# A batched matmul with scale and add: the weight loaded by GpSimd's queue, and GpSimd's DMAs as single packets

## The chip, the core and the metric

The kernel runs on one core of one Trainium2 chip. The metric is the device time in microseconds (us) of one execution; the lower the better. Three runs of the kernel before took 206.86 to 207.15 us, median 207.01 us.

A core has engines that run side by side and meet at semaphores: PE (TensorE, the matmuls), DVE (VectorE), ACT (ScalarE), POOL (GpSimd) and SP (SyncE, which here only issues DMAs). DMAs are carried out by 16 DMA engines that all queues share. A transfer that SP issues goes into one queue (hardware_dynamic in the profile), a transfer that POOL issues into another (software_dynamic). Each DMA engine moves packets; a transfer over 128 partitions is dealt out to the 16 engines.

## What is computed

```python
batch, m, k, n = 16, 512, 1024, 768
out = scale * np.matmul(x, weight) + add_value      # all float32
```

x is 16 x 512 x 1024, weight 1024 x 768, add_value and the result 16 x 512 x 768. Flattened, x has 8192 rows: 64 tiles of 128 rows. The core reads 32 MB of x, 3 MB of weight and 24 MB of addend, and writes 24 MB.

## The kernel before

**Tiles.** A tile t is 128 rows, one on each partition. Four tiles make a *move*; 16 tiles stand in the x buffer `xs` (X_SLOTS), 32 in `ao` (A_SLOTS), which holds the addend of a tile, then its result, until it is stored. At the start the weight lies in float32 in slots 24 to 31 of `ao` (W_AT), which no addend needs yet.

**SP** issues every large DMA in the order of the list `STREAM` (L22 to L29): "x" loads of x, "a" of the addend, "w" of the weight, "o" stores; the numbers are first tile and count. The first x load (tiles 0 to 7, 4 MB) is issued ahead of that, at L239. `sync_engine` (L97) walks the list and puts waits before an entry where it must:
- an x load into used slots waits until ACT and POOL have cast what stood there (`by_act`, `by_pool`, L116 and L117);
- an addend load waits for the addend load before it (`a_sem`, L122). The load of tiles 40 to 47 also waits for `aside_sem` (L126), since slots 8 and 15 of `ao` hold the results of tiles 8 and 15 until POOL has stored them;
- a store waits until DVE has made its tiles (`made`, L142).

SP takes one entry after the other, so a wait holds up all that stand behind it. The weight is issued as two transfers of 1.5 MB, four of the eight chunks of 128 weight rows each. On one partition one such transfer consists of two runs of 6144 bytes, so it has 256 runs, 16 for each DMA engine. An x load of eight tiles is one run of 32768 bytes on a partition, an addend load of eight tiles one of 24576.

**ACT and POOL** run `mover` (L150): they wait for a move's x (L156), wait until a `va` buffer is free (`turned`), and cast x to bfloat16 into `va`, 8 instructions each for a move. Before its loop for moves 0 to 7, POOL does nothing. Between moves 7 and 8 it waits until 16 tiles are made (L246) and issues the three stores of `BY_POOL` by `store_pair` (L93): tiles 8 and 15, of 6, 98 and 24 partitions, each partition two runs of 3072 bytes.

**DVE** (`vector_engine`) first casts the two halves of the weight to bfloat16 (L171), each as soon as it has landed, then transposes the first move (L178). In its loop it alternates between finishing two tiles (L187: scale times product plus addend, in place in `ao`) and transposing half a move into `xt`. A transpose waits for both ACT's and POOL's casts of that move (L175, L176).

**PE** waits for both weight casts (L222) and then goes through the tiles, 16 matmuls each (L210), as fast as `xt` is filled and the results are taken out.

Of the kernel before, what the change touches and what calls it, by code (L numbers as in the profile page):

```python
# [16 lines left out]
VA_BUFS = 2  # L17
MOVE = 4
AHEAD = 4
HALF_BLOCK, PAST, SYNC_AT = 64, 4, 4  # L20

STREAM = [  # L22
# [8 lines left out]
PAIR, TURN_AT = slice(8, 16, 7), 2  # L31
# [4 lines left out]
def kernel(  # L36
# [8 lines left out]
    nc = tc.nc  # L45
# [14 lines left out]
    out_v = out_f.rearrange("(g p t) n -> p g t n", p=P, t=R)  # L60
    w_v = weight.rearrange("(c p r) n -> p c (r n)", p=P, r=2)

    def rows(view, s, n):
        assert s // R == (s + n - 1) // R
        return view[:, s // R, s % R:s % R + n, :]
# [5 lines left out]
    ao = const.tile([P, A_SLOTS, N], fp32, name="ao")  # L71
# [6 lines left out]
    w_sem = [tc.alloc_semaphore(f"w{i}") for i in range(2)]  # L78
    x_sem = [tc.alloc_semaphore(f"x{i}") for i in range(X_SLOTS // MOVE)]
    a_sem = tc.alloc_semaphore("a")  # L80
    o_sem = [tc.alloc_semaphore(f"o{i}") for i in range(2)]
    aside_sem = tc.alloc_semaphore("aside")
# [5 lines left out]
    W_AT = A_SLOTS - KJ  # L88

    def slot(t):  # L90
        return t % A_SLOTS

    def store_pair(eng, p, n):  # L93
        assert PAIR.stop <= R and PAIR.stop <= A_SLOTS
        eng.dma_start(out_v[p:p + n, 0, PAIR, :], ao[p:p + n, PAIR, :]).then_inc(aside_sem, 16)  # L95

    def sync_engine(eng):  # L97
        groups, stores, known = 0, [], {}

        def need(sem, value):  # L100
            if known.get(sem, 0) < value:
                eng.wait_ge(sem, value)  # L102
                known[sem] = value

        for at, (op, s, n) in enumerate(STREAM):
            if at == SYNC_AT:
                eng.addr_align(HALF_BLOCK, offset=PAST, max_nops=0)
            last = s + n - 1
            if op == "w":
                dst = ao[:, W_AT + s:W_AT + s + n, :].rearrange("p (c r) n -> p c (r n)", r=2)  # L110
                move, sem = eng.dma_start(dst, w_v[:, s // 2:(s + n) // 2, :]), w_sem[s // 4]
            elif op == "x":
                k = s % X_SLOTS
                if last >= X_SLOTS:
                    moved = 8 * (last + 1 - X_SLOTS) // MOVE
                    need(by_act, moved)  # L116
                    need(by_pool, moved)  # L117
                move = eng.dma_start(xs[:, k:k + n, :], rows(x_v, s, n))  # L118
                sem = x_sem[k // MOVE]
            elif op == "a":  # L120
                if groups:
                    need(a_sem, 16 * groups)  # L122
                if last == A_SLOTS - 1:
                    need(casts, KJ)
                if s <= PAIR.start + A_SLOTS <= last:
                    need(aside_sem, 16 * len(BY_POOL))  # L126
                if s >= A_SLOTS:
                    i = next(j for j, (a, b) in enumerate(stores) if a <= last - 1 - A_SLOTS < a + b)
                    need(o_sem[i % 2], 16 * (i // 2 + 1))
                move = eng.dma_start(ao[:, slot(s):slot(s) + n, :], rows(add_v, s, n))  # L130
                sem = a_sem
                groups += 1
            elif op == "a+":
                need(a_sem, 16 * groups)
                eng.sem_inc(a_sem, 16 * (n // G - 1))
                groups += n // G - 1
                continue
            else:
                i = len(stores)
                if i > 1:  # L140
                    need(o_sem[i % 2], 16 * (i // 2))
                need(made, MADE + last + 1)  # L142
                move = eng.dma_start(rows(out_v, s, n), ao[:, slot(s):slot(s) + n, :])
                sem = o_sem[i % 2] if s < ENDING else end_sem
                stores.append((s, n))
            move.then_inc(sem, 16)
            if op == "x" and n == 2 * MOVE:
                eng.sem_inc(x_sem[k // MOVE + 1], 16)

    def mover(eng, copy, parity, count, go=None, first=0, turns=T // X_SLOTS):  # L150
        if go is None:
            eng.preload_act_table(mybir.ActivationFunctionType.Copy)  # L152
        with eng.Fori(16 * (first + 1), 16 * (first + turns) + 1, 16) as i:  # L153
            for q in range(X_SLOTS // MOVE):
                eng.wait_ge(x_sem[q], i)
                eng.wait_ge(turned, i + (4 * q - 12) if q < 3 else i)  # L156
                if go is not None:
                    eng.sem_inc(go, 1)  # L158
                k = MOVE * q
                src = xs[:, k:k + MOVE, :].rearrange("p i (c b k) -> p (i c) b k", b=4, k=64)  # L160
                for a in (parity, parity + 2):
                    for b in range(4):
                        copy(va[q % VA_BUFS][32 * b:32 * b + 32, :, a, :],  # L163
                             src[32 * a:32 * a + 32, :, b, :]).then_inc(count, 1)

    def vector_engine(eng):
        ao_g = ao.rearrange("p (g t) n -> p g t n", t=G)

        def cast_w(s, n):
            eng.wait_ge(w_sem[s // 4], 16)  # L170
            eng.tensor_copy(w_bf[:, s:s + n, :], ao[:, W_AT + s:W_AT + s + n, :]).then_inc(casts, n)  # L171

        def turn(move, half, moves=None):
            if half == 0:
                eng.wait_ge(by_act, moves)  # L175
                eng.wait_ge(by_pool, moves)  # L176
            q = 2 * half * KC
            eng.transpose(  # L178
                xt[:, 2 * half:2 * half + 2, :, :].rearrange("p i c m -> p (i c m)"),
                va[move % VA_BUFS][:, q:q + 2 * KC, :, :].bitcast(fp32).rearrange("p c a k -> p (c a k)"),  # L180
            ).then_inc(turned, 2)

        def finish(pair, at, products):
            eng.wait_ge(done, products)
            a = ao_g[:, at, 2 * pair:2 * pair + 2, :]
            q = 2 * (pair % 2)
            eng.scalar_tensor_tensor(  # L187
                a, mm[:, q:q + 2, 0:N], float(scale), a,
                op0=mybir.AluOpType.mult, op1=mybir.AluOpType.add).then_inc(made, 2)

        def group(i, at, last):
            eng.wait_ge(a_sem, i)
            for p in range(4):
                finish(p, at, i + (4 * p - 12) if p < 3 else i)
                if p < 2 or not last:
                    turn(1 if p < 2 else 0, p % 2, i + 8 if p == 2 else i)

        cast_w(0, 4)
        cast_w(4, 4)
        turn(0, 0, 8)  # L200
        turn(0, 1)
        with eng.Fori(16, 2 * T, 16) as i:
            group(i, bass.ds((i // 16 + A_SLOTS // G - 1) % (A_SLOTS // G), 1), False)
        s = slot(T - G) // G
        group(2 * T, slice(s, s + 1), True)
# [12 lines left out]
    def tensor_engine(eng):  # L218
        eng.sem_inc(x_sem[1], 16)
        eng.sem_inc(turned, TURNED)  # L220
        eng.sem_inc(made, MADE)
        eng.wait_ge(casts, KJ)  # L222
        with eng.Fori(TURNED + 2, TURNED + 2 + T, XT_TILES) as i:
            for q in range(XT_TILES):
                if q % 2 == 0:
                    eng.wait_ge(turned, i + q if q else i)
                    eng.wait_ge(made, i + q if q else i)
                for j in range(KJ):
                    x2 = xt[:, q, j // 2, :].bitcast(bf16).rearrange("p (m r) -> p r m", r=2)
                    m = product(eng, mm[:, q, :], x2[:, j % 2, :], w_bf[:, j, :], j)  # L230
                if q % 2:
                    m.then_inc(done, 4)
# [4 lines left out]
    s, n = FIRST  # L237
# [4 lines left out]
    with tc.tile_critical(no_gpsimd_drain=True):  # L242
        sync_engine(nc.sync)
        mover(nc.scalar, nc.scalar.copy, 0, by_act)
        mover(nc.gpsimd, nc.gpsimd.tensor_copy, 1, by_pool, pool_go, 0, TURN_AT)
        nc.gpsimd.wait_ge(made, MADE + PAIR.stop)  # L246
        for p, n in BY_POOL:
            store_pair(nc.gpsimd, p, n)
        nc.gpsimd.addr_align(HALF_BLOCK, offset=PAST, max_nops=0)
        mover(nc.gpsimd, nc.gpsimd.tensor_copy, 1, by_pool, pool_go, TURN_AT, T // X_SLOTS - TURN_AT)  # L250
        vector_engine(nc.vector)
        tensor_engine(nc.tensor)
# [40 lines left out]
```

## Time and profile before

| | us |
|---|---|
| median of 3 runs | 207.01 |
| the profiled execution | 206.85 |
| its span (first to last instruction) | 205.5 |
| PE busy | 167.5 |
| POOL busy | 137.4 |
| ACT busy | 134.7 |
| DVE busy | 98.0 |

HBM traffic is 87.04 MB, 424 GB/s over the span. The times in the views that follow are counted from the start of the span. An engine's busy time is the sum of its instructions. In the lists of DMA issues the last number is the time from issue to landing, which holds the time that a transfer stands in its queue. The chain of waits follows back what released each step, from the last instruction of the program.

### The profile page before, as it was taken

To read this page: it belongs to the slowest core of one execution; us is meant where nothing else is said; L and a number is where in the kernel's file an instruction comes from. 1 tells how busy PE (TensorE), PEld (TensorE's weight loads), DVE (VectorE), ACT (ScalarE), POOL (GpSimd) and SP (SyncE) were. 2 spreads that over 40 slices of the span, in tenths; PEclk is the share of its full clock that TensorE was granted. 3 is DMA by queue.
4 is the path that set the end of the run, shared out by engine and by line. 5 is a ranking of instruction groups with operands and counts; after the bars stand their busy time and mean duration, and the time that the engine had idled before them with its cause. 6 is when DMAs were issued, how large, how long until landed. Compare 5 with 4: busy or idle time off the path is not lost.

```text
span 205.5 us, 2223 instructions
## 1 busy us (share of the span) xinstructions
PE 167.5 (82%) x1008; PEld 50.4 (25%) x512; DVE 98.0 (48%) x66; ACT 134.7 (66%) x129; POOL 137.4 (67%) x135
## 2 busy tenths in 40 slices
PE   0000099999999999999999999999999997999900
PEld 0000022233322333223332233332333322333200
DVE  0004525537555555465555555555552853455330
ACT  2049980699999906999999059999991099920000
POOL 0049994699999916999999549999992099930000
PEclk9999999999999999999999999999999999999995
DMA  8989999999999899999999999999999999998997
GB/s 287 427 372 438 440 485 408 392 437 459 446 459 459 357 459 408 408 426 413 455 404 450 431 416 464 434 411 421 440 431 415 437 448 421 493 459 364 423 440 304
DMA packets 4065, 87.04 MB, mean 424 GB/s; under 512 B 480, under 2 KB 480, under 8 KB 1120
## 3 DMA queue, kind: packets, MB, share of 16 engines
q1 hardware_dynamic: 3856, 86.25, 98.1%
q0 software_dynamic: 208, 0.79, 0.9%
q14 instruction: 1, 0.01, 0.0%
HBM read 61.87 MB, written 25.17 MB: 424 GB/s over the span
## 4 chain that ended last, share of the span: by engine, by line
DMA 38%; PE 36%; POOL 10%; ACT 5%; issue 4%; DVE 3%; SPq 1%; POOLq 0%; DVEq 0%; ACTq 0%
PE mm L210 36%; DMA out_dram<-ao 22%; DMA xs<-in_x_dram 15%; POOL va L163 9%; ACT va L163 5%; DVE xt L178 2%; DVE ao L187 1%; POOL out_dram L95 1%; SPq L130 0%; SPq L118 0%; DVEq L176 0%; SPq L102 0%; POOLq L156 0%; POOLq L158 0%; POOLq L153 0%
## 5 line engine op out<-in xcount | busy, mean ns | idle before, releaser
L210 PE MATMUL mm<-w_bf,xt 128*128 128x256 bf16 (+1 forms) x1008 | 167.5, 327 | 28.0 <-DVE xt L178 27.1
L163 POOL CAST va<-xs 32x1024 bf16<-32x1024 f32 x128 | 135.2, 1056 | 44.2 <-DMA xs<-in_x_dram 36.8
L163 ACT CAST va<-xs 32x1024 bf16<-32x1024 f32 x128 | 133.4, 1042 | 45.2 <-DMA xs<-in_x_dram 42.2
L187 DVE SCALAR_TENSOR_TENSOR ao<-mm,ao 128x1536 f32 (+1 forms) x32 | 56.2, 1756 | 72.9 <-PE mm L210 68.9
L208 PEld LDWEIGHTS <-xt 128*128 128x128 bf16 x512 | 50.4, 98 | 144.6 <-issue 116.6
L178 DVE STREAM_TRANSPOSE xt<-va 128x1024 f32<-128x1024 f32 x32 | 39.4, 1234 | 8.4 <-POOL va L163 6.3
L171 DVE CAST w_bf<-ao 128x3072 bf16<-128x3072 f32 x2 | 4.5, 2240 | 18.1 <-DMA ao<-in_weight_dram 18.1
L152 ACT ACT_TABLE_LOAD x1 | 1.3, 1283 | 1.3 <-SPq L242 1.3
L95 POOL DMA_DIRECT2D out_dram<-ao x3 | 2.0, 672 | 0.0
L274 POOL MEMSET const-float32-0.0<- 128x1 f32 x1 | 0.1, 98 | 0.2 <-issue 0.2
L274 POOL MEMSET const-bfloat16-1.0<- 128x1 bf16 x1 | 0.1, 101 | 0.0
L274 POOL MEMSET const-float32-1.0<- 128x1 f32 x1 | 0.1, 98 | 0.0
L274 POOL MEMSET const-uint8-127<- 128x1 uint8 x1 | 0.1, 98 | 0.0
## 6 DMA issues: line engine op xcount, KB each, us to landing
xs<-in_x_dram SPq DMA_DIRECT2D x7, 4096.0 KB, 20.9
ao<-in_add_value_dram SPq DMA_DIRECT2D x6, 3072.0 KB, 15.7
out_dram<-ao SPq DMA_DIRECT2D x3, 3072.0 KB, 27.4
ao<-in_add_value_dram SPq DMA_DIRECT2D x1, 6144.0 KB, 24.2
out_dram<-ao SPq DMA_DIRECT2D x1, 6144.0 KB, 31.2
out_dram<-ao SPq DMA_DIRECT2D x1, 4608.0 KB, 14.9
xs<-in_x_dram SPq DMA_DIRECT2D x2, 2048.0 KB, 21.0
ao<-in_weight_dram SPq DMA_DIRECT2D x2, 1536.0 KB, 16.8
```

The lines of the kernel that those rows point to most:

```text
L95: eng.dma_start(out_v[p:p + n, 0, PAIR, :], ao[p:p + n, PAIR, :]).then_inc(aside_sem, 16)
L152: eng.preload_act_table(mybir.ActivationFunctionType.Copy)
L163: copy(va[q % VA_BUFS][32 * b:32 * b + 32, :, a, :], src[32 * a:32 * a + 32, :, b, :]).then_inc(count, 1)
L171: eng.tensor_copy(w_bf[:, s:s + n, :], ao[:, W_AT + s:W_AT + s + n, :]).then_inc(casts, n)
L178: eng.transpose(xt[:, 2 * half:2 * half + 2, :, :].rearrange("p i c m -> p (i c m)"), va[move % VA_BUFS][:, q:q + 2 * KC, :, :].bitcast(fp ...
L187: eng.scalar_tensor_tensor(a, mm[:, q:q + 2, 0:N], float(scale), a, op0=mybir.AluOpType.mult, op1=mybir.AluOpType.add).then_inc(made, 2)
L208: eng.ldweights(x_j, tile_position=(0, 0))
L210: m = eng.add_instruction(mybir.InstMatmult(start_tensor_calc=(j == 0), stop_tensor_calc=(j == KJ - 1), tile_size=(P, P), tile_position=(0 ...
L274: nc = _bacc.Bacc("TRN2", target_bir_lowering=False, num_devices=1)
```

## The change

SP's list loses its two weight entries. POOL issues the same two transfers to the same places, at the head of its program: after it has seen the first x load land, and before its first cast. Both of them, and the three stores of tiles 8 and 15, carry a flag, `single_packet`, that asks for one packet on each DMA engine that a transfer uses. `SYNC_AT`, a position in the list at which SP's code is aligned, moves with the list by two, so that it stays at the same entry.

```diff
-HALF_BLOCK, PAST, SYNC_AT = 64, 4, 4
+HALF_BLOCK, PAST, SYNC_AT = 64, 4, 2

 STREAM = [
-    ("w", 0, 4), ("w", 4, 4), ("a", 0, 8),
+    ("a", 0, 8),
     ("x", 8, 8), ("a", 8, 8), ("x", 16, 8), ("a", 16, 16), ("x", 24, 8),
...
     def store_pair(eng, p, n):
         assert PAIR.stop <= R and PAIR.stop <= A_SLOTS
-        eng.dma_start(out_v[p:p + n, 0, PAIR, :], ao[p:p + n, PAIR, :]).then_inc(aside_sem, 16)
+        eng.dma_start(out_v[p:p + n, 0, PAIR, :], ao[p:p + n, PAIR, :], single_packet=True).then_inc(aside_sem, 16)
+
+    def load_weight(eng):
+        for s in (0, 4):
+            dst = ao[:, W_AT + s:W_AT + s + 4, :].rearrange("p (c r) n -> p c (r n)", r=2)
+            eng.dma_start(dst, w_v[:, s // 2:s // 2 + 2, :], single_packet=True).then_inc(w_sem[s // 4], 16)
...
-            if op == "w":
-                dst = ao[:, W_AT + s:W_AT + s + n, :].rearrange("p (c r) n -> p c (r n)", r=2)
-                move, sem = eng.dma_start(dst, w_v[:, s // 2:(s + n) // 2, :]), w_sem[s // 4]
-            elif op == "x":
+            if op == "x":
...
         mover(nc.scalar, nc.scalar.copy, 0, by_act)
+        nc.gpsimd.wait_ge(x_sem[0], 16)
+        load_weight(nc.gpsimd)
         mover(nc.gpsimd, nc.gpsimd.tensor_copy, 1, by_pool, pool_go, 0, TURN_AT)
```

## The prediction

> **What bounds the kernel now.** I read the table of DMA queues first, because section 2 of the page shows the DMA row at 9 in nearly every slice. Its columns are packets, MB and share of 16 engines' span.
>
> ```profile
> q1 hardware_dynamic: 3856, 86.25, 98.1%
> q0 software_dynamic: 208, 0.79, 0.9%
> out_dram<-ao SPq DMA_DIRECT2D x1, 6144.0 KB, 31.2
> out_dram<-ao SPq DMA_DIRECT2D x1, 4608.0 KB, 14.9
> ao<-in_weight_dram SPq DMA_DIRECT2D x2, 1536.0 KB, 16.8
> out_dram<-ao POOLq DMA_DIRECT2D x1, 588.0 KB, 15.1
> out_dram<-ao POOLq DMA_DIRECT2D x1, 144.0 KB, 18.7
> out_dram<-ao POOLq DMA_DIRECT2D x1, 36.0 KB, 7.4
> ```
>
> The two data queues together fill 99.0% of the 16 engines. The bytes set the time, as long as SP's queue never runs dry. The other lines are issues with their time to landing. Next, the timeline of the start: what do the first 26 us wait for? Columns: start, length, engine, line, instruction, and in brackets the idle time before it.
>
> ```profile
> 0.74 0.38 SPq L239 DMA_DIRECT2D xs<-in_x_dram  x1
> 1.39 0.90 SPq L111 DMA_DIRECT2D ao<-in_weight_dram  x2
> 12.89 17.04 ACT L163 CAST va<-xs 32x1024 bf16<-32x1024 f32 x16 [10.26 <-DMA xs<-in_x_dram]
> 13.04 20.27 POOL L163 CAST va<-xs 32x1024 bf16<-32x1024 f32 x16 [12.60 <-DMA xs<-in_x_dram]
> 16.65 2.31 DVE L171 CAST w_bf<-ao 128x3072 bf16<-128x3072 f32 x1 [16.65 <-DMA ao<-in_weight_dram]
> 20.40 2.17 DVE L171 CAST w_bf<-ao 128x3072 bf16<-128x3072 f32 x1 [1.44 <-DMA ao<-in_weight_dram]
> 24.69 2.37 DVE L178 STREAM_TRANSPOSE xt<-va 128x1024 f32<-128x1024 f32 x2 [2.12 <-ACT va L163]
> 26.00 34.27 PE L210 MATMUL mm<-w_bf,xt 128*128 128x512 bf16 x197 [26.00 <-DVE xt L178]
> 27.64 0.33 SPq L130 DMA_DIRECT2D ao<-in_add_value_dram  x1
> 33.41 0.33 SPq L118 DMA_DIRECT2D xs<-in_x_dram  x1
> 37.44 23.45 ACT L163 CAST va<-xs 32x1024 bf16<-32x1024 f32 x22 [7.51 <-DMA xs<-in_x_dram]
> 44.67 0.33 SPq L130 DMA_DIRECT2D ao<-in_add_value_dram  x1
> ```
>
> Transfers land in order: x of move 0 and 1 at 12.8, the weight halves at 16.6 and 20.4, tiles 0 to 7 of the addend at 27.6 (SP waits for them before it issues at 27.64), x 8 to 15 at 37.4. PE starts at 26.0, behind a transpose that waited for casts, not for the weight: DVE was idle for 2.12 us after the second weight cast. So the weight may land about 2 us later before PE moves.
>
> The waits of PE from 150 us on show one single stall, and the timeline of the end (DVE, then PE, then SP) says where PE's progress meets the queue.
>
> ```profile
> PE mm L210 <- DVE xt L178: 1.1, 1, 1.1
> 185.17 1.76 DVE L187 SCALAR_TENSOR_TENSOR ao<-mm,ao 128x1536 f32<-128x1536 f32 x1 [1.98 <-PE mm L210]
> 174.49 20.97 PE L210 MATMUL mm<-w_bf,xt 128*128 128x512 bf16 x126 [1.13 <-DVE xt L178]
> 159.64 38.10 SPq L143 DMA_DIRECT2D out_dram<-ao  x3
> ```
>
> Store 32-47 is issued at 159.64 and lands 31.2 later, at 190.84. Store 48-59 needs tile 59, which DVE makes at 185.17 + 1.76 = 186.93. It is issued 3.9 us before the queue would run dry. That is the smallest reserve in the kernel: all later bytes hang on it, and PE's progress sets it.
>
> **The change, part by part.**
>
> *Fewer packets.* The second weight half took 20.40 − 16.65 = 3.75 us in the hardware queue; the addend tiles behind it, of twice its bytes in packets of 24 KB, took 27.64 − 20.40 = 7.24, or 3.62 per 1.5 MB. I put the 0.13 us between them down to 16 packets of 6 KB per engine (256 runs over 16 engines) instead of one: 9 ns a packet. Two halves give −0.26. The stores of tiles 8 and 15 go from up to 10 data packets on an engine to 3: −0.06. Sum **−0.32 us** of engine time; 0 if the cost is one per run and not per packet, which is the other end.
>
> *Two transfers leave SP's queue.* SP issues the addend at about 1.4 instead of 2.3 us, behind an x load that keeps the engines busy to 12.8: nothing. The same bytes must pass before 27.6 either way, so the addend's landing stays, and with it the issue at 27.64. If it came late, x 8 to 15, landing at 37.4, covers 9.7 us.
>
> *Two issues on POOL.* The wait on x_sem[0] is the one its first cast has already, so it adds no time. Behind it stand both transfers and then the 16 casts of moves 0 and 1.
>
> ```profile
> L95 POOL DMA_DIRECT2D out_dram<-ao x3: 596/693/727, 96.2 to 97.6; - x3
> L163 POOL CAST va<-xs x10: 1026/1034/2452, 13.0 to 25.7; 32x1024 bf16<-32x1024 f32 x10
> ```
>
> One issue takes 0.60 to 0.73 us, hardly more for 98 partitions than for 6. So POOL's casts start 1.4 us later. Alone that would push PE from 26.0 to about 27.4. The slots that they free go to the x load issued at 33.41; it would go at 34.8, with cover up to 44.67, when the addend before it lands.
>
> *When the weight lands.* This decides. Three facts come from the one place where POOL stores while SP's queue is full. These are tables of DMA queues for 96 to 100, 100 to 101 and 103 to 108 us:
>
> ```profile
> q1 hardware_dynamic: 92, 1.70, 99.1%
> q14 instruction: 1, 0.01, 0.5%
> ...
> q0 software_dynamic: 2, 0.00, 0.1%
> ...
> q1 hardware_dynamic: 71, 1.74, 81.0%
> q0 software_dynamic: 73, 0.37, 17.7%
> 96.23 2.01 POOL L95 DMA_DIRECT2D out_dram<-ao  x3
> ```
>
> The last line is POOL's timeline: first issue at 96.23. No packet of its queue moves before 100 us, and only two tiny ones before 101: about 4.7 us until the engines take up POOL's queue. Then packets alternate one to one (71 to 73), and both queues together stay full. Third, the 36 KB store has one data packet on an engine and yet lands only after 7.4 us, which fits a count (semaphore) packet with a turn of its own.
>
> For the weight: wait done 12.9; + 4.7 = 17.6; + 0.45, half an addend packet (7.24 / 8 = 0.9); + 3.6 for the first half, 98 KB on each engine in one piece; + 0.9 for SP's turn; + 3.6 for the second half = 26.1. If the count has its own turn after each half, add 0.9 and 1.2 (an x packet: 9.7 / 8). Neither form is in the trace; I take the middle, +1.05: **second half at 27.2**. The ends: the start delay could be as short as that of the first x load at an idle chip, whose packets move from the second microsecond on.
>
> ```profile
> 0.00:1.00 1.00, 0.00 (x0) 0.00 (x0) 0.00 (x0) 0.00 (x0) 0.20 (x4) 1.00 0.00 0
> 1.00:2.00 1.00, 0.00 (x0) 0.00 (x0) 0.00 (x0) 0.66 (x1) 0.00 (x0) 1.00 1.58 426
> 0.74 12.05 DMA xs<-in_x_dram
> ```
>
> (The last two columns of the first two rows, from the table of 1 us windows, are DMA share and GB/s; the third row is from the chain.) That gives 1.0 us, so 12.9 + 1.0 + 3.6 + 0.9 + 3.6 = 22.0; the late end is 28.7. I stay near 4.7, the row of POOL's own queue under load. [...]
>
> *From the weight to the end.* Weight cast 2.17, transpose 1.26 (half of 2.37 with overlap) and gaps of 0.2 follow: PE starts at 27.2 + 3.6 = 30.8, **4.8 us later**. PE has had one stall since, of 1.13; it swallows that much, so tile 59 is made 3.7 us later and store 48-59 goes out at 190.6 instead of 186.9. A queue that starts from empty loses time: the first x load took 12.05 us, an x load within the stream 37.44 − 27.64 = 9.8, so 2.3; its first packets came after 1.0; I take 1.7. Data flows at 192.3 where it flowed at 190.84: **+1.45**. From there the rest runs as before, so the −0.32 ahead of it is lost in the hole. Sum: +1.45 on 206.85 (span 205.5 + 1.35 around it) = 208.3; the median of the runs shown, 207.01, is 0.16 above the profiled one: **208.4 us**.
>
> *Stalls in between.* Two issues could also run dry under a late PE.
>
> ```profile
> 78.84 17.45 POOL L163 CAST va<-xs 32x1024 bf16<-32x1024 f32 x16 [6.30 <-DMA xs<-in_x_dram]
> 120.68 34.96 POOL L163 CAST va<-xs 32x1024 bf16<-32x1024 f32 x32 [4.95 <-DMA xs<-in_x_dram]
> 97.65 18.69 DMA out_dram<-ao
> ```
>
> POOL stands idle 6.3 and 4.95 us for x at these two places, so the casts that free slots are done that much ahead, and x is what they wait for, not PE. The last row is the store of tiles 8 and 15, whose landing at 116.34 releases SP for the addend of tiles 40 to 47. With three data packets on an engine it should land some 8 us earlier. That brings nothing: x 40 to 47 fills the queue until 120.6, and what SP issues then waits behind it. If that cover were gone it would be worth up to 4 us.
>
> **The rivals.**
> - *The weight lands in time (not slower).* Place: POOL's queue at 13 us. If its packets are taken up within about 2 us and the counts ride in the packets, the second half lands by 24, PE starts at 27.6, and 1.6 − 1.13 = 0.5 eats into the 3.9 of reserve. Then only −0.32 stays: 206.7. It decides from PE starting at 26 + 1.1 + 3.9 − 1.7 = 29.3 on, a landing by 25.7. [...] Against it: the 4.7. [...]
> - *Later still.* 4.7 us, counts in turns of their own, a full packet's wait: 28.7, PE at 32.3, tile 59 5.2 later, store at 192.1, restart 2.3: data at 194.4, +3.6: 210.6.
> - *One packet per engine does not come about.* Then 32 pieces of 6 KB each wait for a packet of 24 or 32 KB: 32 × (0.23 + 0.9 to 1.2) = 36 to 46 us, PE starts at about 60, and with PE's 169.5 us to its end and 10 more the time is near 240. Against it: nothing in the trace; the stores already went in 128 data packets for 256 runs, so several runs do fit in one.
>
> **How the numbers follow.** Forecast, with the hole between 0.4 and 2.5 us: 0.47, 207.4 to 209.5. In time: 0.33. Later still: 0.17. No single packet: 0.03. The range takes the second and most of the third: 206.5 to 210.4. A measurement of this kernel can tell 0.2% (0.4 us) from no change. The case "in time" lies at that edge: 0.17 of it goes to faster, 0.16 to same; the rest, 0.67, is slower.
>
> **What would show it.** In the profile after: the first packet of POOL's queue near 17.6; DVE's second weight cast near 27 and not before 25; its start is the test of the whole chain. PE's first matmul near 30.8; no PE stall near 173; store 48-59 issued after 190 and a window with low DMA share just behind it. Wrong would be: the second weight cast before 25.7; or a hole elsewhere, for instance before x 32 to 39; or a queue of SP that slows beyond its bytes while a 98 KB packet holds an engine.

## The result and the profile after

The changed kernel takes 235.38 us (median of 5 runs, 234.93 to 235.85) against 207.01: ratio 1.1373, 95% interval 1.136 to 1.1387. Its profiled execution took 234.98 us with a span of 233.6, so 28.1 us more span than before.

The page of the changed kernel, its DMA queues (packets, MB, share of 16 engines) and its issues (KB each, us from issue to landing):

```profile
span 233.6 us, 2239 instructions
DMA  7999999995993088039999999999999999999798
...
q1 hardware_dynamic: 3312, 83.10, 84.3%
q0 software_dynamic: 752, 3.93, 4.0%
...
ao<-in_weight_dram POOLq DMA_DIRECT2D x2, 1536.0 KB, 32.3
```

Before, SP's queue had 3856 packets and POOL's 208; now 3312 and 752. What SP lost, POOL gained, one for one: 544 packets, which is 512 for the weight and 32 counts. (A count is here a packet under 512 bytes at the end of a transfer: the table of the changed kernel for 72 to 82 us has 16 packets, all of them under 512 bytes, as many as there are engines.) So the profile counts as many packets as before, and nothing was joined. And the DMA row, which was full throughout (8 or 9 in every slice but the last), falls to 5 in its tenth slice and has holes in slices 13, 14, 17 and 18; a slice is 5.84 us.

The timelines of the changed kernel, POOL's, DVE's, PE's and the last line of DVE's (start, length, engine, line, instruction, idle time before it):

```profile
13.15 1.59 POOL L100 DMA_DIRECT2D ao<-in_weight_dram  x2 [12.71 <-DMA xs<-in_x_dram]
14.79 17.44 POOL L165 CAST va<-xs 32x1024 bf16<-32x1024 f32 x16
37.38 1.76 DVE L173 CAST w_bf<-ao 128x3072 bf16<-128x3072 f32 x1 [37.38 <-DMA ao<-in_weight_dram]
54.48 1.76 DVE L173 CAST w_bf<-ao 128x3072 bf16<-128x3072 f32 x1 [15.34 <-DMA ao<-in_weight_dram]
57.45 168.61 PE L212 MATMUL mm<-w_bf,xt 128*128 128x512 bf16 x1024 [57.45 <-DVE xt L180]
226.16 1.76 DVE L189 SCALAR_TENSOR_TENSOR ao<-mm,ao 128x1536 f32<-128x1536 f32 x1 [3.44 <-PE mm L212]
```

The weight halves are in at 37.4 and 54.5 us, where they were in at 16.6 and 20.4. PE starts 31.45 us late. From there it runs without a stall to 226.06, 168.6 us; it needed 169.5 from its start before, with its stall of 1.13. Behind it come 7.5 us instead of 10.0, because the last store has less in front of it: the store ahead lands some 2.0 us after the last one's issue (217.6 + 12.4, issued at 228.0), where it was 4.5 (187.0 + 14.9, issued at 197.4). The last store lands 5.6 us after its issue, where it took 8.1. 31.45 − 0.9 − 2.5 = 28.1: the late start accounts for the whole loss.

Three DMA tables of the changed kernel, for 14 to 17, 17 to 18 and 22 to 32 us, show the place.

```profile
q1 hardware_dynamic: 54, 1.33, 103.1%
...
q1 hardware_dynamic: 14, 0.34, 79.8%
q0 software_dynamic: 16, 0.10, 23.4%
...
q1 hardware_dynamic: 107, 3.31, 76.8%
q0 software_dynamic: 117, 0.72, 17.1%
```

Up to 17 us POOL's queue moves no packet. From 22 to 32 us the two queues move about as many packets (107 and 117), but SP's are x packets of 32768 bytes and POOL's are weight packets of 6144. POOL gets half the turns and 0.72 of 4.03 MB. From 17 to 54.5 us, the whole time of the weight, the DMA table has:

```profile
q1 hardware_dynamic: 482, 12.37, 76.9%
q0 software_dynamic: 544, 3.15, 20.1%
```

The 544 are the whole weight with its counts, 34 packets for each of the 16 engines; SP's 482 are 30 for each. The two queues together filled 97% of the engines' time, and four fifths of that went to SP's bytes. The holes in the DMA row come later and are consequences. SP's own waits from 50 to 104 us (us in total, times, longest):

```profile
SPq L107 <- POOL va L165: 45.7, 2, 25.3
SPq L107 <- DVE w_bf L173: 23.5, 1, 23.5
```

SP could not load addend tiles 16 to 31 before the weight was cast out of slots 24 to 31, nor x 24 to 31 and 32 to 39 before POOL had cast what stood in those slots. The table of stretches has an 8 us one inside such a hole (after the times: PE busy, PEld, DVE, ACT, POOL, clock, DMA share, GB/s):

```profile
74.00:82.00 8.00, 8.00 (x51) 2.44 (x25) 4.30 (x3) 7.56 (x8) 7.55 (x8) 1.00 0.00 0
```

The DMA engines move nothing there while PE is fully busy. In the chain of waits PE has 72% and DMA 22%, where it was 36% and 38%: DMA is no longer what sets the end.

### The profile page after: what moved, and what is told of

The parts are those of the page before. It is cut to its first block, busy times and chain, and to the rows that moved or that the text cites. A ratio compares the mean times of both kernels' runs of the same rounds, so it can differ in the third digit from the quotient of the medians.

```text
span 233.6 us, 2239 instructions
## 1 busy us (share of the span) xinstructions
PE 168.6 (72%) x1024; PEld 50.4 (22%) x512; DVE 96.6 (41%) x66; ACT 134.7 (58%) x129; POOL 136.1 (58%) x137
## 3 DMA queue, kind: packets, MB, share of 16 engines
q1 hardware_dynamic: 3312, 83.10, 84.3%
## 4 chain that ended last, share of the span: by engine, by line
PE 72%; DMA 22%; DVE 1%; issue 1%; POOL 0%; DVEq 0%; POOLq 0%
PE mm L212 72%; DMA ao<-in_weight_dram 17%; DMA xs<-in_x_dram 5%; DVE ao L189 1%; DVE xt L180 1%; POOL ao L100 0%; DVEq L204 0%; DVE w_bf L173 0%; DVEq L186 0%; POOLq L158 0%; POOLq L155 0%; DVEq L172 0%; POOLq L160 0%
## 5 line engine op out<-in xcount | busy, mean ns | idle before, releaser
L212 PE MATMUL mm<-w_bf,xt 128*128 128x512 bf16 (+1 forms) x1024 | 168.6, 328 | 57.5 <-DVE xt L180 57.5
L165 POOL CAST va<-xs 32x1024 bf16<-32x1024 f32 x128 | 132.4, 1034 | 60.6 <-DVE xt L180 35.7
L173 DVE CAST w_bf<-ao 128x3072 bf16<-128x3072 f32 x2 | 3.5, 1760 | 52.7 <-DMA ao<-in_weight_dram 52.7
L100 POOL DMA_DIRECT2D ao<-in_weight_dram x2 | 1.6, 797 | 12.7 <-DMA xs<-in_x_dram 12.7
## 6 DMA issues: line engine op xcount, KB each, us to landing
out_dram<-ao SPq DMA_DIRECT2D x1, 4608.0 KB, 12.4
```

The source lines that it names most:

```text
L100: eng.dma_start(dst, w_v[:, s // 2:s // 2 + 2, :], single_packet=True).then_inc(w_sem[s // 4], 16)
L165: copy(va[q % VA_BUFS][32 * b:32 * b + 32, :, a, :], src[32 * a:32 * a + 32, :, b, :]).then_inc(count, 1)
L212: m = eng.add_instruction(mybir.InstMatmult(start_tensor_calc=(j == 0), stop_tensor_calc=(j == KJ - 1), tile_size=(P, P), tile_position=(0 ...
```

## The experiments

Theory A, the author's reading of the 71 and 73 packets that the two queues moved from 103 to 108 us in the kernel before and of the 544 that were not joined: a DMA engine takes one packet of each queue in turn, whatever the packets' sizes, and the flag joins nothing. Then 32 weight packets and their counts on each engine wait for as many packets of SP's. The rivals are that the flag itself slows the queue, that POOL's software queue is served badly, that the late start or the wait costs the time, and that queues share by bytes. Each ratio below is to runs of the kernel before that were taken with it. The first of these kernels was timed 4 times, the second 11 times, the last 12 times and every other one twice.

**No flag.** The changed kernel without `single_packet`:

```diff
-... ao[p:p + n, PAIR, :], single_packet=True).then_inc(aside_sem, 16)
+... ao[p:p + n, PAIR, :]).then_inc(aside_sem, 16)
-... w_v[:, s // 2:s // 2 + 2, :], single_packet=True).then_inc(w_sem[s // 4], 16)
+... w_v[:, s // 2:s // 2 + 2, :]).then_inc(w_sem[s // 4], 16)
```

> The changed kernel without the one-packet flag on any of the five transfers. Theory A (each queue gets one packet in turn on a DMA engine; the flag does not join packets here): nothing changes. 235.4 us within 0.5, 640 data packets of 6144 bytes in the software queue, second weight cast at 54.5 us, one cast near 37.4. [...]

235.04 us, ratio to the kernel before 1.1349 (1.1331 to 1.1368). POOL's queue again has 640 packets of 6144 bytes. DVE's timeline of this run:

```profile
54.42 1.76 DVE L173 CAST w_bf<-ao 128x3072 bf16<-128x3072 f32 x1 [15.34 <-DMA ao<-in_weight_dram]
```

0.06 us from the changed kernel's. The flag neither causes the loss nor softens it.

**Flag on the stores alone.** The kernel before with the flag in `store_pair`:

```diff
-... ao[p:p + n, PAIR, :]).then_inc(aside_sem, 16)
+... ao[p:p + n, PAIR, :], single_packet=True).then_inc(aside_sem, 16)
```

> The kernel before with the flag on the three stores of tiles 8 and 15 alone. Theory A (the flag joins nothing): 207.0 us within 0.2%, the stores land after about 7, 15 and 18 us as before, 128 data packets of 6144 bytes. Rival (the flag joins the packets of one engine): the 98-partition store lands after 8 us or less with 32 data packets, and the time falls by about 0.06 us.

207.11 us, ratio 0.9997 (0.9988 to 1.0006). The DMA queues and issues of this run:

```profile
q0 software_dynamic: 208, 0.79, 0.9%
...
out_dram<-ao POOLq DMA_DIRECT2D x1, 588.0 KB, 14.4
out_dram<-ao POOLq DMA_DIRECT2D x1, 144.0 KB, 17.6
out_dram<-ao POOLq DMA_DIRECT2D x1, 36.0 KB, 6.8
```

208 packets as before, and landings 0.6 to 1.1 us ahead of before's 15.1, 18.7 and 7.4. The last experiment below, which has no flag, has 14.6, 17.9 and 7.0, so the difference need not be the flag's. This part of the change does nothing that these runs can tell.

**ACT issues the weight.** The same place and time, but in ACT's hardware queue, and no flag:

```diff
+        nc.scalar.wait_ge(x_sem[0], 16)
+        load_weight(nc.scalar)
         mover(nc.scalar, nc.scalar.copy, 0, by_act)
-        nc.gpsimd.wait_ge(x_sem[0], 16)
-        load_weight(nc.gpsimd)
```

> The changed kernel with the two weight transfers issued by ACT instead of POOL, at the same place (after the first x load has landed, ahead of ACT's casts), without the flag. Theory A (any second queue gets one packet for each packet of SP's queue): 32 weight packets and 2 count packets take about as long as in the changed kernel, second half in at 50 to 55 us, time 230 to 235 us. Rival (POOL's software queue alone is served badly): second half in by about 24 us, time below 209 us.

235.37 us, ratio 1.1363 (1.134 to 1.1385). ACT's queue is q10. This run's DMA table for 22 to 32 us:

```profile
q1 hardware_dynamic: 110, 3.51, 81.2%
q10 hardware_dynamic: 113, 0.69, 16.5%
```

And DVE's timeline:

```profile
54.43 1.76 DVE L173 CAST w_bf<-ao 128x3072 bf16<-128x3072 f32 x1 [15.53 <-DMA ao<-in_weight_dram]
```

The same alternation, the same end. It is not POOL's queue alone that is slow: ACT's moves 113 packets beside SP's 110, as POOL's moves 117 beside 107, small packets in a second queue beside large ones in a first.

**Half the weight.** The first half back in SP's list ahead of the addend, only the second by POOL:

```diff
-    ("a", 0, 8),
+    ("w", 0, 4), ("a", 0, 8),
...
-        for s in (0, 4):
+        for s in (4,):
```

> The changed kernel with the first weight half back at its old place in SP's queue; only the second is POOL's. Theory A (one packet of POOL's for one of SP's): 16 data packets and one count packet from 17.3 us on: 7 turns beside addend packets (1.15 us each), 8 beside x packets (1.45), 1 more and the count: in at 39 us, PE starts at 42, and with 168.6 us of PE, 7.5 of tail and 1.35 around the span 219.5 us. Rival C (the delay is POOL's late start, not the number of packets): second half in by 25 us, 207 to 209 us.

218.32 us, ratio 1.0549 (1.0451 to 1.0646). The second half was in at 37.6 us, PE started at 40.60. Rival C, a landing by 25, is out: issued at 13.1 us as in the changed kernel, half the packets land 24.4 us after their issue instead of 40.4. With the changed kernel's first packet behind 17 us that is some 20 us instead of 37, an estimate.

**Fewer, larger packets.** Four neighbouring rows on a partition (12288 bytes) in two transfers, or eight (24576 bytes) in one. The diff is of the first; the second has r=8 and a single `dma_start`, for which both casts wait:

```diff
-    w_v = weight.rearrange("(c p r) n -> p c (r n)", p=P, r=2)
+    w_v = weight.rearrange("(c p r) n -> p c (r n)", p=P, r=4)
...
-            eng.dma_start(dst, w_v[:, s // 2:s // 2 + 2, :], ...
+            eng.dma_start(dst, w_v[:, s // 4:s // 4 + 1, :], ...
```

> The changed kernel with four neighbouring weight rows on a partition, so that a transfer is 128 runs of 12288 bytes (product of the reordered weight). The same bytes in half the packets. Theory A (turns, not bytes): 18 turns from 17.3 us, each longer by 0.23: second half in at 43 us, PE starts at 46.5, 224 us. Rival D (the queues share by bytes or time): second half in at 54 us as in the changed kernel, 235 us. If the flag joins packets after all: in by 30 us.

> The changed kernel with eight neighbouring weight rows on a partition and one transfer of 128 runs of 24576 bytes (product of the reordered weight); both casts then wait for this one transfer. Theory A (one packet for one packet): 8 data packets and one count from 17.4 us, 3 beside addend packets (0.91 + 0.91 us), 5 beside x packets (0.91 + 1.21), 1.2 for the count: in at 34.7 us; PE starts at 39.7 after two casts in a row; 217 us. By bytes alone it would land at 54 us as in the changed kernel, 236 us.

Both kernels leave out putting x's columns into the new order of the weight's rows, so they compute the product of another weight; the bytes that are moved stay the same.

222.04 us, ratio 1.0728 (1.0676 to 1.0781), and 216.4 us, ratio 1.0454 (1.0424 to 1.0485). DVE's timelines, first of the 12288-byte kernel, then of the 24576-byte one:

```profile
41.83 1.76 DVE L173 CAST w_bf<-ao 128x3072 bf16<-128x3072 f32 x1 [9.48 <-DMA ao<-in_weight_dram]
```

```profile
33.55 3.43 DVE L172 CAST w_bf<-ao 128x3072 bf16<-128x3072 f32 x2 [33.55 <-DMA ao<-in_weight_dram]
```

The same 3 MB in 32, 16 and 8 packets on an engine are all in at 54.5, 41.8 and 33.6 us, from an issue at 13.1 to 13.3. Sharing by bytes, which would have left all three near 54, is out here. These two and the half before them landed 1.1 to 1.4 us ahead of what was written down; that is taken up behind the next two experiments.

**SP's packets halved, POOL's left alone.** The x loads of tiles 8 to 15 and 16 to 23 as four loads of four tiles:

```diff
-    ("x", 8, 8), ("a", 8, 8), ("x", 16, 8), ("a", 16, 16), ("x", 24, 8),
+    ("x", 8, 4), ("x", 12, 4), ("a", 8, 8), ("x", 16, 4), ("x", 20, 4), ("a", 16, 16), ("x", 24, 8),
```

> The changed kernel with the x loads of tiles 8 to 15 and 16 to 23 each issued as two loads of four tiles, so that SP's x packets in that stretch are 16384 bytes and not 32768. POOL's weight packets are as they were. Theory A (each weight packet waits for one packet of SP's, whatever its size): the turns beside x fall from 1.45 to 0.85 us; 3 addend turns to 20.8, 16 x turns to 34.4, 8 addend turns to 43.6, 7 x turns: second half in at 49.5 us instead of 54.4, PE starts at 52.6, 229.5 us. If POOL's queue has a fixed rate or a share of the bytes: 54.4 us and 235 us as before.

227.96 us, ratio 1.1012 (1.098 to 1.1044). DVE's timeline, and the DMA table for 22 to 32 us:

```profile
46.62 1.76 DVE L173 CAST w_bf<-ao 128x3072 bf16<-128x3072 f32 x1 [12.82 <-DMA ao<-in_weight_dram]
...
q1 hardware_dynamic: 207, 3.13, 73.1%
q0 software_dynamic: 204, 1.16, 27.6%
```

The weight came 7.9 us sooner though nothing of it or of POOL was touched; 4.9 were expected. POOL's queue moved 204 packets in these 10 us, where it moved 117 in the changed kernel. So in these two runs POOL's queue has no rate of its own: it goes with the size of SP's packets.

**No wait for x.** POOL issues the weight near 2 us, ahead of the first x load's landing:

```diff
-        nc.gpsimd.wait_ge(x_sem[0], 16)
         load_weight(nc.gpsimd)
```

> The changed kernel without POOL's wait for the first x load: the weight is issued in the first microsecond. Theory A: the 34 turns start at about 4 us, beside x packets: second half in at 48 us, PE starts at 51, 228 us; the first x load lands at 14 to 15 us instead of 12.8. Rival E (the wait for the first x load is what costs the time): below 212 us.

226.55 us, ratio 1.0947 (1.0903 to 1.099); second weight cast at 46.0, PE from 48.98. Issued 11.2 us earlier, the weight is in 8.5 us earlier. The wait costs part of the loss, not most of it. The first x load pays for it: ACT's first cast starts at 14.60 us, where it started at 12.89.

In the last five kernels the weight landed ahead of what was written down: by 1.4 us (half), 1.2 (12288 bytes), 1.1 (24576 bytes), 2.9 (SP's halved) and 2.0 (no wait). The estimates took each packet of SP's that one of POOL's stands beside for a data packet. In these stretches 2, 2, 1, 4 and 4 of SP's packets on an engine are its counts, by the transfers that end there (the changed kernel's table for 17 to 54.5 us has 96 packets under 512 bytes, 32 of the weight's and 64 of SP's, so 4 on an engine). If a turn beside one of these is short, that fits the misses; this is the author's estimate, and no run separates it.

**POOL alone.** SP holds the addend back until both halves are in:

```diff
             last = s + n - 1
+            if at == 0:
+                need(w_sem[0], 16)
+                need(w_sem[1], 16)
             if op == "x":
```

> The changed kernel with SP waiting for both weight halves before it issues the addend, so that POOL's queue has the engines to itself. Theory A: no turns to wait for, both halves in 7.6 us: first packet 1.5 to 4.2 us after the issue at 13.15, second half in at 22.5 to 25 us, PE starts at 26 to 28.5. The engines are idle for 2 to 4.5 us at 13 and about 2 us after, so 211 to 213.5 us. If the delay of 4.2 us to POOL's first packet is due to the load of the engines: first packet by 15 us; if it is fixed: 17.3.

213.23 us, ratio 1.0303 (1.0263 to 1.0343). POOL's and DVE's timelines:

```profile
13.35 1.59 POOL L100 DMA_DIRECT2D ao<-in_weight_dram  x2 [12.90 <-DMA xs<-in_x_dram]
20.18 1.84 DVE L176 CAST w_bf<-ao 128x3072 bf16<-128x3072 f32 x1 [20.18 <-DMA ao<-in_weight_dram]
23.92 1.76 DVE L176 CAST w_bf<-ao 128x3072 bf16<-128x3072 f32 x1 [1.90 <-DMA ao<-in_weight_dram]
```

The DMA tables of this run for 13.1 to 14.5 and for 14.5 to 15.5 us:

```profile
DMA packets 0, 0.00 MB, mean 0 GB/s; under 512 B 0, under 2 KB 0, under 8 KB 0
...
q0 software_dynamic: 16, 0.10, 68.4%
```

Without a competitor the second half takes 23.92 − 20.18 = 3.74 us, as fast as in SP's queue before (3.75). POOL's first packets come 1.2 to 2.2 us after its issue, against at least 3.9 (13.15 to beyond 17) in the changed kernel: in these two runs the delay goes with the load, no packet from 13.1 to 14.5 us here and a share of 103.1% from 14 to 17 there. DVE's first instruction starts at 20.18 us here and at 37.38 there, so DVE's work does not make the difference. The kernel still loses, since the engines stand idle around the weight: from 12 to 27 us the DMA share is 0.69, against 1.02 in the kernel before. By that some 5 of the 6.7 us of additional span are lost there, an estimate; the rest was not traced.

**Larger packets in SP's queue.** The kernel before with rows four by four, to measure the price of a packet:

```diff
-    w_v = weight.rearrange("(c p r) n -> p c (r n)", p=P, r=2)
+    w_v = weight.rearrange("(c p r) n -> p c (r n)", p=P, r=4)
```

> The kernel before with four neighbouring weight rows on a partition instead of two times two, so that one transfer is 128 runs of 12288 bytes; the weight's rows then stand in another order than x's columns, and the product is of the reordered weight. Packets of the weight fall from 32 to 16 on an engine. By the packet price of the prediction (9 ns): -0.14 us, ratio 0.9993. If the price is by byte only: 0. If larger runs also read faster from HBM: more than -0.3 us.

This kernel, too, computes the product of a reordered weight. 207.07 us, ratio 1.0002 (0.9991 to 1.0013). In the profile the second half took 20.41 − 16.73 = 3.68 us, against 3.76 (20.48 − 16.72) in the flag-on-stores run, where the weight is loaded as before: 0.08 for 8 fewer packets, 10 ns each, one profile of each. At the end 0.14 us cannot be told from nothing.

**The kernels whose weight moved, in one table**, in us from the profiles. The second column counts the weight's data packets on a DMA engine that stand beside SP's; the last column is span minus PE's start:

| kernel | packets beside SP's | second weight cast | PE starts | span | rest |
|---|---|---|---|---|---|
| before | none | 20.40 | 26.00 | 205.5 | 179.5 |
| POOL alone | none | 23.92 | 28.02 | 212.2 | 184.2 |
| 24576 bytes | 8 | 33.55 (both) | 38.19 | 215.1 | 176.9 |
| half | 16 | 37.62 | 40.60 | 216.2 | 175.6 |
| 12288 bytes | 16 | 41.83 | 44.80 | 220.3 | 175.5 |
| no wait | 32 | 46.01 | 48.98 | 224.9 | 175.9 |
| SP's halved | 32 | 46.62 | 49.59 | 226.6 | 177.0 |
| no flag | 32 | 54.42 | 57.40 | 233.0 | 175.6 |
| ACT's queue | 32 | 54.43 | 57.40 | 234.1 | 176.7 |
| changed | 32 | 54.48 | 57.45 | 233.6 | 176.2 |

Wherever PE starts at 38 us or later, the rest is 175.5 to 177.0: PE sets the end and the start sets the time. Where it starts at 26 or 28 the rest is longer: PE stalls for 1.13 us in the kernel before and for 4.80 in POOL alone (2.85, 0.18, 0.38 and 1.39). With 98.1% of the engines' time in SP's queue in the kernel before, that is put down to DMA. None of the versions beats the kernel before.

## Why the prediction was wrong

The forecast was 208.4 us, range 206.5 to 210.4; measured 235.38.

- **The step that failed** is "3.6 for the first half, 98 KB on each engine in one piece", and the same for the second. The flag joined nothing: the runs without it and with it on the stores alone showed the same packets and times. In place of 3.6 + 0.9 + 3.6 stood 32 pieces of 6 KB, each beside a packet of SP's: 37 us from 17.3 to 54.4, where the sum had 8.1. Why the flag joins nothing here stays open.
- The right case was on the list, the rival "one packet per engine does not come about", with 36 to 46 us and "near 240". It got a chance of 0.03. The argument against it was the 128 data packets for 256 runs of the stores. Those were packets formed *without* the flag. That row showed that two runs of 3072 bytes on one partition shared a packet; it said nothing of what the flag adds, and no row did. For the weight itself the same profile spoke against it: its 512 runs of 6144 bytes were 512 packets in SP's queue, two for each partition and transfer. A step that the whole sum hung on had no row, and deserved far more than 0.03.
- **The alternation**, one packet for one, read from 71 to 73, was right as far as the packets go (482 to 544, or 30 to 34 for each engine, over the whole stretch), and it is what makes the rival's price come out. From 22 to 32 us the changed kernel's queues moved 107 and 117 packets, those of ACT's run 110 and 113, and those of the run with SP's halved 207 and 204. What takes a turn here is a packet as the profile counts it, one weight run of 6144 bytes.
- **The delay to POOL's first packet** was right: forecast at 17.6, the first 16 packets moved between 17 and 18. The lower end of 1.0 us was near what idle DMA engines gave in POOL alone (1.2 to 2.2).
- **POOL's issue time** was right: 1.59 us for two, forecast 1.4, and nothing hung on it, since PE waited for the weight.
- **The packet price** came out near (9 ns forecast, 10 measured), but its row was misread: 1.5 MB of addend are four packets of 24 KB on an engine and not one, so the 0.13 us stand for 12 packets, 11 ns each. The −0.32 never arose, since no packet was saved. The stores of tiles 8 and 15 landed 1 to 2 us sooner after their issue (16.6 against 18.7 for the last), not 8, and not by the flag: in ACT's run, without it, the last took 16.0.
- **From the weight to PE** (+3.6 forecast, 57.45 − 54.48 = 3.0 measured) and PE's stall being swallowed were right. The restart of an empty queue behind store 32-47 did not set the time, so the term of +1.45 was not tested: with PE this late, the queue was dry long before (a DMA share of 0.00 from 74 to 82 us), and PE's own 168.6 us set the end.

## What to carry to other kernels

In these runs a second DMA queue shared the engines by packets and not by bytes (107 and 117 packets, 3.31 and 0.72 MB, from 22 to 32 us of the changed kernel). So, before moving a transfer to another queue, count its packets on an engine and multiply by the size of the packets that they will stand beside. Here the small packets were better off in the queue of the large ones, ahead of what could wait (207.01 us against 235.38), where they cost their own bytes (3.75 us for 1.5 MB). And where a flag carries the whole plan, look for a row in which it acts, or give the case that it does nothing a real chance.

## What was not expected of the hardware

`single_packet` left packets and times as they were, and landings about as in runs without it, for stores of 3072-byte runs (208 packets with it and without) and loads of 6144-byte runs (640 packets in POOL's queue, second weight cast at 54.48 us with it and 54.42 without) alike. Halving the packets of one queue sped up the other: the weight came in 7.9 us sooner when only SP's x loads were cut in two. And the delay from issue to first packet of POOL's queue was 1.2 to 2.2 us on idle engines (POOL alone) and 3.9 or more beside a full queue (the changed kernel).
